# A state-space stage with its rotation sums on TensorE, merged products and phase rounding on ScalarE

## The chip, the cores and the metric

The kernel runs on one core of a Trainium2 chip. The metric is the device time of one execution in microseconds (us). Engines are written PE (TensorE matmul), PEld (TensorE weight load), DVE (VectorE), ACT (ScalarE), POOL (GpSimd) and SP (SyncE, which issues most DMAs). ACT and POOL issue some DMAs too; each engine works through its own instructions in order, so an instruction that waits holds up all that stand behind it on that engine.

## The reference, cut to what matters

The whole is a two-layer trunk of 256 time steps with 2048 channels: a state-space mixer with a gated linear unit (GLU) and a convolutional feed-forward network, then latent attention and a second feed-forward network. The change lies in the state-space mixer alone:

```
def s5_mixer(u, ...):                       # 128 groups of 16 channels, 64 complex states each
    mag = exp(dt * a_re)
    ab = mag * (cos(dt * a_im) + i sin(dt * a_im))
    bb = ((ab - 1) / a) * b
    h[t] = ab * h[t-1] + bb @ u[t]          # per group, complex, 256 steps
    y[t] = Re(c @ h[t]) + d_skip * u[t]
    y = gelu(y)
    val, gate = split(y @ w_glu + b_glu)
    return val * sigmoid(gate)
```

All of it is in 32-bit floating point. The numerators of `bb` and the output factors enter as products of powers of `ab` with `b` and `c`.

## The kernel before

The state-space stage (function `s5`) treats the 128 groups in 16 blocks of 8. Within a block, time is cut into 32 pieces of 8 steps; one piece times 16 channels makes the 128 rows of a tile. Inside a piece the recurrence is a matrix product with a 128 x 128 Toeplitz matrix; between pieces the state is carried by a scan over 32 positions. The complex state is rotated by the phase of each piece first, so that the scan runs with the real magnitude alone, and rotated back afterwards.

One pass of the loop at L610 to L645 works on several blocks at once. For pass n it does, in the order of the code:

- `part_v(n-1)` (L431): U times the transposed first-stage factors ET give each piece's contribution to the state; ScalarE copies it out of PSUM into `vs` (the copies follow L527).
- `part_c(n-2)` (L431 again, tiles `TP,U` and `f,H`): the output sums, U times the Toeplitz tile TP plus the state H times the output factors f. Per group pair there are three terms: U by TP, H by f1, H by f2.
- `part_r(n-1)`: four transposes (L530, L531) put the state and its swapped halves into PSUM; L533 and L534 multiply them by the cosine and the sine frame (`co`, `si`), L535 adds, L541 is the scan whose result is R.
- `part_k(n)`: U (L483), the block's kernel sums K from f and the loaded factors bc (L431, tiles `f,bc`), the skip diagonal (L438), a copy of K to DRAM (`kd`, on ScalarE's queue) and from there four loads in Toeplitz form (TP, L503, on SyncE's queue).
- `fetch(n+3)` (L460): the factor tile bc of a later block, 256 KB on ScalarE's queue, three buffers.
- `part_e(n)` (L514): eight transposes of the first-stage factors e.
- `part_h(n-1)`: a matmul with a swap matrix (L546) exchanges the halves of R in PSUM; L548 multiplies R by the cosine, L549 the swapped R by the sine, and L555 subtracts: H, written into columns 1 to 31 of each 32.
- `lead_f(n+1)`: the two output-factor products f1 and f2 (L454, 1024 elements a partition each), and in every second block the frames: L412 multiplies phase by position, L413 rounds by adding and taking off a large constant, L414 subtracts the rounded part, then Abs, Sin, Sin on ScalarE (L415 to L417).
- `lead_e(n+2)`: the two first-stage products e (L454 too), summed by an accumulating DMA from GpSimd (L468). Every fourth block `powers` (up to L405) makes the power factors `zs` for four blocks, which four ScalarE copies lay out.

Between these pieces `advance` puts steps of the GLU product of the blocks that are already done: 24 matmuls of 512 columns each (L254, L255, L257), with ScalarE and VectorE splitting the weights into two parts (L76, L77) and VectorE adding partial sums (L280). The first such step follows the fourth block; GLU weights come in 1 MB loads on SyncE's queue. `part_d` applies Gelu (L582) and transposes (L586) every four blocks.

The order of the instructions on each engine is not that of the code: a scheduler in the framework decides it when the program is built. A tile's buffer count, given with the tile, sets when it may be written again. The products are DVE's, the sums PE's; what links them here is H, which PE needs in `part_c` of the following pass, and f, which waits for the last reader of its buffer, `part_c` of three blocks earlier.

Of the kernel before, what the change touches and what calls it, by code (L numbers as in the profile page):

```python
# [47 lines left out]
def tile_trunk(ctx: ExitStack, tc: tile.TileContext, a: dict):  # L48
# [234 lines left out]
    def s5(f):  # L283
        with tc.tile_pool(name="s5", bufs=2) as q1, tc.tile_pool(name="dr", bufs=2, space=bass.MemoryType.DRAM) as dr:
# [61 lines left out]
            for K in Ks:  # L346
                pool.memset(K[:, 2 * P :], 0.0)
            Ds = [T(q1, [P, 8, 32], F32, f"dc{i}", 1) for i in range(2)]
# [32 lines left out]
            def powers(qt):  # L381
                ps_ = slice(32 * qt, 32 * qt + 32)
                z = T(q1, [P, 2, 9, 2, 32], F32, "z", 1)
                pool.memset(z[:, 0, 8, 1, :], 1.0)
                pool.memset(z[:, 1, 8, 1, :], 0.0)
                act.activation(z[:, :, 8, 0, :], cf[:, :, ps_], AF.Copy)
                act.activation(z[:, :, 0, 1, :], L[8][:, :, ps_], AF.Copy)
                for k, o, i, m in ((1, 7, 8, 1), (2, 5, 7, 2), (4, 1, 5, 4)):

                    def v(b):  # L390
                        return z[:, :, b : b + m].rearrange("p c m t n -> p c (m t) n")

# [8 lines left out]
                zz = T(q1, [P, 4, 8, 32], F32, "zs")  # L401
                act.activation(zz[:, 1], z[:, 1, 0:8, 1, :], AF.Copy, scale=cst[:, C_SG : C_SG + 1])
                act.activation(zz[:, 2], z[:, 0, 1:9, 0, :], AF.Copy, scale=cst[:, C_NSG : C_NSG + 1])
                act.activation(zz[:, 3], z[:, 1, 1:9, 0, :], AF.Copy, scale=-1.0)
                act.activation(zz[:, 0], z[:, 0, 0:8, 1, :], AF.Copy)  # L405
                return zz

            def frames(k):
                ps_ = slice(FR * NP * k, FR * NP * (k + 1))
                m, n = T(q1, [P, FR * NP, 32], F32, "si"), T(q1, [P, FR * NP, 32], F32, "co")  # L410
                cv = cst[:, C_CV : C_CV + 32].unsqueeze(1).to_broadcast([P, FR * NP, 32])
                dve.tensor_tensor(m, th[:, ps_].unsqueeze(2).to_broadcast([P, FR * NP, 32]), cv, op=ALU.mult)  # L412
                dve.tensor_scalar(n, m, MAGIC, MAGIC, op0=ALU.add, op1=ALU.subtract)  # L413
                dve.tensor_tensor(m, m, n, op=ALU.subtract)  # L414
# [3 lines left out]
                return [z.rearrange("p (k n) c -> k p (n c)", k=FR) for z in (m, n)]  # L418
# [31 lines left out]
            def product(tag, bufs, sb, i):  # L450
                h = (sb % PB) * NP
                o = T(q1, [P, NP, 8, 16], F32, tag, bufs)
                zt = zs[sb // PB][:, i, :, h : h + NP].rearrange("p i n -> p n i").unsqueeze(3).to_broadcast([P, NP, 8, 16])
# [8 lines left out]
            def lead_e(n):  # L462
# [4 lines left out]
                E[n], e2 = product("e1", 3, n, 0), product("e2", 2, n, 1)  # L467
                pool.dma_start(E[n], e2, accum_op=ALU.add)  # L468

            def lead_f(n):  # L470
                if n >= nb:
                    return
                F[n] = product("f1", 3, n, 2), product("f2", 3, n, 3)
                if n % FR == 0:
                    si, co = frames(n // FR)
                    for k in range(FR):
                        fr[n + k] = (si[k], co[k])
# [47 lines left out]
            def part_r(sb, vs, si, co):  # L525
# [6 lines left out]
                w1, w2 = T(q1, [P, W], F32, "w1"), T(q1, [P, W], F32, "w2")  # L532
                dve.tensor_tensor(w1, pvt, co, op=ALU.mult)  # L533
                dve.tensor_tensor(w2, pvs, si, op=ALU.mult)  # L534
                dve.tensor_tensor(w1, w1, w2, op=ALU.add)  # L535
# [8 lines left out]
            def part_h(sb, R, si, co):  # L544
# [3 lines left out]
                dve.tensor_tensor(h1, R, co, op=ALU.mult)  # L548
                dve.tensor_tensor(h2, prs, si, op=ALU.mult)  # L549
# [5 lines left out]
                dve.tensor_tensor(H[:, :, 1:32], cc(h1), cc(h2), op=ALU.subtract)  # L555
                return H

            def part_c(sb, yg, ff, U, TP, H):
                def h(g, j):
                    return H[:, 4 * g + j, :]  # L560
# [3 lines left out]
                    *((h, lambda g, j, z=z: flat2(z[:, 4 * g + j])) for z in ff),  # L564
# [31 lines left out]
            todo, zs, bc, E, F, fr, U, TP, ET, H = [], {}, {}, {}, {}, {}, {}, {}, {}, {}  # L596
# [13 lines left out]
            for n in range(nb + 2):  # L610
# [7 lines left out]
                if 0 <= n - 1 < nb:  # L618
                    R = part_r(n - 1, vs, *fr[n - 1])
# [14 lines left out]
                if 0 <= n - 1 < nb:  # L634
                    H[n - 1] = part_h(n - 1, R, *fr.pop(n - 1))
# [628 lines left out]
```

## Time and profile before

| what | value |
|---|---|
| median of 3 runs | 2123.69 us (2121.5 to 2124.83) |
| the profiled execution's own time | 2123.76 us |
| its span, first to last instruction | 2122.0 us |
| mean granted TensorE clock | 0.990 |
| busy over the span: PE, PEld | 2045.2 us, 1754.5 us |
| busy over the span: DVE, ACT, POOL | 1375.1 us, 1091.3 us, 31.0 us |
| DMA moved | 392.15 MB, mean 185 GB/s |
| share of the chain that ended last: PE, DVE, DMA, ACT | 88%, 5%, 3%, 2% |

The state-space stage is the first 236 us of the span or so. Its scans stand at 43.6, 53.3, 69.7, 78.9 and 86.0 us (blocks 0 to 4), then at 106.9, 117.8, 129.9, 146.1, 162.6, 172.8, 184.3, 194.7, 210.0, 218.5 and 229.3 us. A row of a timeline gives start, length, engine, line, operation, the tile written and the tiles read, shape and count; a length is that of a pipelined operation, so the step from one row's start to the next is what it costs on a busy engine. On PE one fp32 matmul of the 32-column-wide form is two records, so x16 stands for eight matmuls. An entry `[4.25 <-DVE H L555]` is idle time of the engine just before, and what ended it. A row of the windows view gives, for one stretch, each engine's busy time with its instructions in brackets, then the granted clock, the busy share of the DMA engines and the GB/s. A row of waits gives the sum of the waiting time, the number of waits and the longest.

### The profile page before, as it was taken

How to read it: one execution, taken by the hardware profiler on the slowest of the kernel's cores; microseconds unless marked ns; L12 is line 12 of the kernel's file. 1: busy time of each engine (PE TensorE's matmuls, PEld its weight loads, DVE VectorE, ACT ScalarE, POOL GpSimd, SP SyncE). 2: the span in 40 equal slices, each digit the busy share in tenths (PEclk: the TensorE clock that was granted, in tenths of full speed). 3: DMA queues.
4: the chain of work that ended last, by engine and by line, in shares of the span. 5: the costliest groups of instructions: out<-in, count | busy, mean ns of one | idle time of the engine just before them, and what ended most of it. 6: DMA issues, size and time to landing. Idle time of an engine off the chain costs nothing.

```text
span 2122.0 us, 30720 instructions
## 1 busy us (share of the span) xinstructions
PE 2045.2 (96%) x12372; PEld 1754.5 (83%) x12372; DVE 1375.1 (65%) x1935; ACT 1091.3 (51%) x1680; POOL 31.0 (1%) x73
## 2 busy tenths in 40 slices
PE   3789999999999999999999999999999999999998
PEld 2567788988888888888888998898888888888886
DVE  8889677665566556656785666656546655665566
ACT  6565456554455345534564555555445544554453
POOL 1000000000000000000000000000000000000000
PEclk9899999999999999999999999999999999999999
DMA  5777775755565565556444445475555655555642
GB/s 148 199 189 212 244 254 166 250 187 180 199 197 179 185 200 190 179 196 197 139 149 163 125 144 177 163 257 186 187 201 181 196 181 198 184 194 179 198 159 80
DMA packets 292255, 392.15 MB, mean 185 GB/s; under 512 B 10256, under 2 KB 205456, under 8 KB 291600
## 3 DMA queue, kind: packets, MB, share of 16 engines
q1 hardware_dynamic: 285632, 374.45, 53.7%
q0 software_dynamic: 2304, 8.39, 2.3%
q10 hardware_dynamic: 4176, 7.34, 1.0%
q8 instruction: 97, 1.59, 0.3%
q14 instruction: 46, 0.38, 0.1%
HBM read 375.73 MB, written 6.03 MB: 180 GB/s over the span
## 4 chain that ended last, share of the span: by engine, by line
PE 88%; DVE 5%; DMA 3%; ACT 2%; issue 1%; POOL 0%; SPq 0%; ACTq 0%; DVEq 0%; POOLq 0%
PE wk L758 29%; PE wk L760 15%; PE acc L115 9%; PE acc L114 9%; PE acc L113 9%; PE wk L113 2%; PE wk L114 2%; PE wk L115 2%; PE acc L255 2%; PE acc L254 2%; PE acc L257 2%; PE wk L431 2%; PE wk L255 1%; PE wk L257 1%; PE wk L254 1%
## 5 line engine op out<-in xcount | busy, mean ns | idle before, releaser
L77 DVE TENSOR_TENSOR wlo<-raw,whi 128x1024 fp32r<-128x1024 f32 (+1 forms) x590 | 699.6, 1188 | 543.7 <-ACT whi L76 540.3
L76 ACT ACTIVATE whi<-raw 128x1024 fp32r<-128x1024 f32 (+1 forms) x590 | 605.8, 1029 | 667.0 <-PE wk L758 298.5
L758 PE MATMUL wk<-act,whi 128*128 128x512 f32 x2688 | 674.0, 393 | 0.0
L758 PEld LDWEIGHTS wk<-act,whi 128*128 128x128 f32 x2688 | 484.6, 189 | 86.3
L760 PEld LDWEIGHTS wk<-act,wlo 128*128 128x128 f32 x2688 | 366.9, 191 | 26.1
L760 PE MATMUL wk<-act,wlo 128*128 128x256 f32 x2688 | 375.0, 283 | 0.0
L115 PE MATMUL acc<-whi,hl 128*128 128x512 f32 x636 | 249.8, 394 | 0.0
L114 PE MATMUL acc<-wlo,hh 128*128 128x512 f32 x636 | 249.4, 392 | 0.0
L113 PE MATMUL acc<-whi,hh 128*128 128x512 f32 x636 | 247.1, 389 | 0.0
L114 PEld LDWEIGHTS acc<-wlo,hh 128*128 128x128 f32 x636 | 119.5, 188 | 27.5
L113 PEld LDWEIGHTS acc<-whi,hh 128*128 128x128 f32 x636 | 119.5, 188 | 26.4 <-ACT hh L76 0.5
L115 PEld LDWEIGHTS acc<-whi,hl 128*128 128x128 f32 x636 | 119.9, 188 | 23.9
L830 DVE SCALAR_TENSOR_TENSOR cv<-gs,cw,cv 128x255 f32<-128x255 f32 (+1 forms) x168 | 81.0, 482 | 17.2 <-ACT cv L828 14.2
L828 ACT ACTIVATE cv<-gs,cb,cw 128x256 f32<-128x256 f32 x84 | 49.9, 594 | 45.6 <-DVE gs L766 45.6
L254 PE MATMUL acc<-whi,act 128*128 128x512 f32 x156 | 65.5, 420 | 3.8 <-ACT act L76 3.8
L77 DVE TENSOR_TENSOR wlo<-x,whi 128x1024 fp32r<-128x1024 f32 x40 | 48.8, 1223 | 26.7 <-ACT whi L76 26.0
L255 PE MATMUL acc<-whi,act 128*128 128x512 f32 x156 | 63.0, 404 | 1.1 <-DVE act L77 1.1
L76 ACT ACTIVATE whi<-x 128x1024 fp32r<-128x1024 f32 x40 | 42.3, 1061 | 37.6 <-PE wk L758 16.4
L114 PE MATMUL acc<-wlo,act 128*128 128x512 f32 (+1 forms) x152 | 55.0, 362 | 1.0 <-DVE wlo L106 0.9
L113 PE MATMUL acc<-whi,act 128*128 128x512 f32 (+1 forms) x152 | 54.1, 358 | 0.3 <-ACT whi L105 0.3
L115 PE MATMUL acc<-whi,act 128*128 128x512 f32 (+1 forms) x152 | 54.0, 356 | 0.0
L257 PE MATMUL acc<-wlo,act 128*128 128x512 f32 x156 | 49.2, 397 | 0.0
(314 smaller groups left out, 2558.1 us busy)
## 6 DMA issues: line engine op xcount, KB each, us to landing
raw<-in_w_up SPq DMA_DIRECT2D x86, 1024.0 KB
raw<-in_w_gate SPq DMA_DIRECT2D x84, 1024.0 KB
raw<-in_w_down SPq DMA_DIRECT2D x84, 1024.0 KB
raw<-in_w_glu SPq DMA_DIRECT2D x21, 1024.0 KB
x<-in_w_glu SPq DMA_DIRECT2D x11, 1024.0 KB
raw<-in_w_o SPq DMA_DIRECT2D x9, 1024.0 KB
e<-e POOLq DMA_DIRECT2D x16, 512.0 KB, 6.1
TP<-kd SPq DMA_DIRECT2D x64, 128.0 KB
```

What stands on the lines that cost most here:

```text
L76: act.activation(hi, src, AF.Copy)
L77: (eng or dve).tensor_tensor(lo, src, hi.bitcast(F32), op=ALU.subtract)
L113: pe.matmul(o, lh, rh, start=first, stop=False)
L114: pe.matmul(o, lh, rl, start=False, stop=False)
L115: pe.matmul(o, ll, rh, start=False, stop=last)
L254: pe.matmul(bank, ah, wh[:, k, :], start=first and k == 0, stop=False)
L255: pe.matmul(bank, al, wh[:, k, :], start=False, stop=False)
L257: pe.matmul(bank, acts(tb, 4 * b + j + k)[0], wl[:, k, :], start=False, stop=last and k == hk - 1)
L758: pe.matmul(o, w, pair(kt), start=kt == 0, stop=False)
L760: pe.matmul(o[:, 0, :], w, pair(kt)[:, 0], start=False, stop=kt == KT - 1)
L828: act.activation(cv[:, ft, :], gv[:, ft, :], AF.Identity, scale=cw[:, 2, n : n + 1], bias=cb[:, n : n + 1])
L830: dve.scalar_tensor_tensor(cv[:, ft, sh:], gv[:, ft, : S - sh], cw[:, 2 - sh, n : n + 1], cv[:, ft, sh:], op0=ALU.mult, op1=ALU.add,)
```

## The change

Four things are rewritten in `s5`.

1. The difference that made H is no longer taken on VectorE. H becomes two tiles, R times cosine and the swapped R times sine, and the output sums have four terms of f by H in place of two. The minus sign goes into the swap matrix, negated once by ScalarE (`swap`).
2. `part_r` multiplies both PSUM halves by both frames in one operation of 512; `si` and `co` stand in one tile `cs` for that.
3. f1 and f2 come from one operation of 2048 (tag `f1`); the power factors `zs` are laid out by block for that, and ScalarE's copies write them in that layout. The e products stay two operations (`single`).
4. The frames are cut in two. `angles` (phase by position on VectorE, then ScalarE adds the rounding constant, Identity with bias and scale -1) stands in `lead_f`; `frames` (one VectorE operation in place of L413 and L414, then Abs, Sin, Sin) stands in `lead_r` of the following pass.

```diff
-            Hs = [T(q1, [P, 8, 32], F32, f"H{i}", 1) for i in range(2)]
-            for z in Ds + Hs:
+            Hs = [[T(q1, [P, 8, 32], F32, f"H{i}{k}", 1) for k in range(2)] for i in range(2)]
+            swap = T(q1, [P, P], F32, "swap", 1)
+            act.activation(swap, cst[:, C_PS : C_PS + P], AF.Copy, scale=-1.0)
+            for z in Ds + [z for pair in Hs for z in pair]:
...
-            def frames(k):
...
-                dve.tensor_tensor(m, th[:, ps_].unsqueeze(2).to_broadcast([P, FR * NP, 32]), cv, op=ALU.mult)
-                dve.tensor_scalar(n, m, MAGIC, MAGIC, op0=ALU.add, op1=ALU.subtract)
-                dve.tensor_tensor(m, m, n, op=ALU.subtract)
+            def angles(k):
+                both = T(q1, [P, FR, 2, NP * 32], F32, "cs")
...
+                act.activation(n, m, AF.Identity, bias=magic, scale=-1.0)
+                return both, m, n
+
+            def frames(both, m, n):
+                dve.scalar_tensor_tensor(m, n, MAGIC, m, op0=ALU.subtract, op1=ALU.add)
                 act.activation(n, m, AF.Abs)
                 act.activation(m, m, AF.Sin, scale=cst[:, C_TPI : C_TPI + 1])
                 act.activation(n, n, AF.Sin, bias=half_pi, scale=-TWO_PI)
...
             def product(tag, bufs, sb, i):
+                o = T(q1, [P, 2 * NP, 8, 16], F32, tag, bufs)
...
-                E[n], e2 = product("e1", 3, n, 0), product("e2", 2, n, 1)
+                E[n], e2 = single("e1", 3, n, 0), single("e2", 2, n, 1)
...
-                F[n] = product("f1", 3, n, 2), product("f2", 3, n, 3)
+                F[n] = product("f1", 3, n, 2)
                 if n % FR == 0:
-                    si, co = frames(n // FR)
+                    an[n // FR] = angles(n // FR)
+
+            def lead_r(n):
+                if n < nb and n % FR == 0:
+                    both = frames(*an.pop(n // FR))
...
-                w1, w2 = T(q1, [P, W], F32, "w1"), T(q1, [P, W], F32, "w2")
-                dve.tensor_tensor(w1, pvt, co, op=ALU.mult)
-                dve.tensor_tensor(w2, pvs, si, op=ALU.mult)
-                dve.tensor_tensor(w1, w1, w2, op=ALU.add)
+                w = T(q1, [P, 2, W], F32, "w", 1)
+                dve.tensor_tensor(w, pvv.rearrange("p (i w) -> p i w", i=2), cs, op=ALU.mult)
+                w1 = w[:, 0]
+                dve.tensor_tensor(w1, w1, w[:, 1], op=ALU.add)
...
-                pe.matmul(prs, cst[:, C_PS : C_PS + P], R, start=True, stop=True)
-                h1, h2 = T(q1, [P, W], F32, "w1"), T(q1, [P, W], F32, "w2")
-                dve.tensor_tensor(h1, R, co, op=ALU.mult)
-                dve.tensor_tensor(h2, prs, si, op=ALU.mult)
+                pe.matmul(prs, swap, R, start=True, stop=True)
...
-                dve.tensor_tensor(H[:, :, 1:32], cc(h1), cc(h2), op=ALU.subtract)
+                dve.tensor_tensor(H[0][:, :, 1:32], cc(R), cc(cs[:, 0]), op=ALU.mult)
+                dve.tensor_tensor(H[1][:, :, 1:32], cc(prs), cc(cs[:, 1]), op=ALU.mult)
...
-                    *((h, lambda g, j, z=z: flat2(z[:, 4 * g + j])) for z in ff),
+                    *((h(i), lambda g, j, z=z: flat2(z[:, 4 * g + j])) for z in ff for i in range(2)),
...
                     ET[n] = part_e(E.pop(n))
+                    lead_r(n)
```

What the scheduler makes of it is seen in the built order of two engines. The names end in numbers that tell one tile of a kind from the next; they run differently in the two programs. First TensorE, where block 6's output sums stand behind the next block's `part_v` (`ET,U`), before the change:

```order
L431 MATMUL wk_1378<-ET_1303,U_1270 32x128 x8
L431 MATMUL wk_1390<-TP_1114,U_1088 32x128 x4
L431 MATMUL wk_1390<-f_225_1002,H_49_190 32x128 x4
L431 MATMUL wk_1390<-f_226_1004,H_49_190 32x128 x4
L431 MATMUL wk_1390<-TP_1114,U_1088 32x128 x4
L431 MATMUL wk_1390<-f_225_1002,H_49_190 32x128 x4
L431 MATMUL wk_1390<-f_226_1004,H_49_190 32x128 x4
```

And the same place after it:

```order
L446 MATMUL wk_1420<-ET_1355,U_1322 32x128 x8
L446 MATMUL wk_1432<-TP_1153,U_1127 32x128 x4
L446 MATMUL wk_1432<-f_205_1034,H_50_192 32x128 x4
L446 MATMUL wk_1432<-f_205_1034,H_51_193 32x128 x4
L446 MATMUL wk_1432<-f_205_1034,H_50_192 32x128 x4
L446 MATMUL wk_1432<-f_205_1034,H_51_193 32x128 x4
L446 MATMUL wk_1432<-TP_1153,U_1127 32x128 x4
L446 MATMUL wk_1432<-f_205_1034,H_50_192 32x128 x4
L446 MATMUL wk_1432<-f_205_1034,H_51_193 32x128 x4
L446 MATMUL wk_1432<-f_205_1034,H_50_192 32x128 x4
L446 MATMUL wk_1432<-f_205_1034,H_51_193 32x128 x4
```

Sixteen matmuls of f by H stood in a block and 32 do now; the place in the order is the same.

Then VectorE around the scan of block 10, whose result is R (the order calls the scan SCALAR_TENSOR_TENSOR). Before, `e_437` is the second product of block 13, from a tile bc that ScalarE fetched one pass earlier:

```order
L534 TENSOR_TENSOR w_411_1942<-wk_1936,si_1688 128x256
L454 TENSOR_TENSOR f_432_2029<-zs_1874,bc_1617 128x1024
L535 TENSOR_TENSOR w_410_1941<-w_410_1941,w_411_1942 128x256
L454 TENSOR_TENSOR f_433_2031<-zs_1874,bc_1617 128x1024
L541 SCALAR_TENSOR_TENSOR R_1947<-dc_47_188,w_410_1941 128x256
L413 TENSOR_SCALAR co_2034<-si_2033 128x512
L548 TENSOR_TENSOR w_430_2024<-R_1947,co_1689 128x256
L414 TENSOR_TENSOR si_2033<-si_2033,co_2034 128x512
L454 TENSOR_TENSOR e_437_2043<-zs_1874,bc_1801 128x1024
L549 TENSOR_TENSOR w_431_2025<-wk_2022,si_1688 128x256
L280 TENSOR_TENSOR f_84<-acc_2008,f_84 128x512
L555 TENSOR_TENSOR H_49_190<-w_430_2024,w_431_2025 128x8x31
```

After it, `H_50` is R times cosine, `H_51` the swapped R times sine, and `e_413` and `e_414` are the products of block 14, from the tile bc_2069:

```order
L470 TENSOR_TENSOR f_385_2112<-zs_1946,bc_1686 128x2048
L559 TENSOR_TENSOR w_2029<-wk_2024,cs_1752 128x512
L561 TENSOR_TENSOR w_2029<-w_2029 128x256
L567 SCALAR_TENSOR_TENSOR R_2033<-dc_48_190,w_2029 128x256
L578 TENSOR_TENSOR H_50_192<-R_2033,cs_1752 128x8x31
L476 TENSOR_TENSOR e_413_2284<-zs_1946,bc_2069 128x1024
L579 TENSOR_TENSOR H_51_193<-wk_2108,cs_1752 128x8x31
L280 TENSOR_TENSOR f_84<-acc_2094,f_84 128x512
L476 TENSOR_TENSOR e_414_2286<-zs_1946,bc_2069 128x1024
```

The tile bc_2069 is fetched by ScalarE (L482) in this very pass, after that pass's kernel sums; the first product of block 14 now stands between the two halves of H. The other blocks whose scans have the numbers 5 to 11 are like it, with both e products between the halves in most. Of ScalarE's order one row is gone from the end of the stage: the table load ahead of the last Gelu.

More of the change, by code (lines that the diff above doesn't have):

```diff
@@ L400, in powers @@
                     dve.tensor_tensor(v(o)[:, 1], u[:, 1], w[:, 0], op=ALU.add)
[L401 to L405, printed above, removed]
+                zz = T(q1, [P, PB, 4, NP, 8], F32, "zs")
@@ new lines, in blocks, with factor @@
+                def blocks(v):
+                    return v.rearrange("p i (b n) -> p i b n", b=PB)
+                def factor(t):
+                    return zz[:, :, t].rearrange("p b n i -> p i b n")
+                act.activation(factor(1), blocks(z[:, 1, 0:8, 1, :]), AF.Copy, scale=cst[:, C_SG : C_SG + 1])
+                act.activation(factor(2), blocks(z[:, 0, 1:9, 0, :]), AF.Copy, scale=cst[:, C_NSG : C_NSG + 1])
+                act.activation(factor(3), blocks(z[:, 1, 1:9, 0, :]), AF.Copy, scale=-1.0)
@@ L406, in powers @@
+                act.activation(factor(0), blocks(z[:, 0, 0:8, 1, :]), AF.Copy)
                 return zz
-            def frames(k):
+            def angles(k):
                 ps_ = slice(FR * NP * k, FR * NP * (k + 1))
[L410 to L414, printed above, removed]
+                both = T(q1, [P, FR, 2, NP * 32], F32, "cs")
+                n, m = (both[:, :, i].rearrange("p k (n c) -> p k n c", c=32) for i in range(2))
+                cv = cst[:, C_CV : C_CV + 32].unsqueeze(1).unsqueeze(1).to_broadcast([P, FR, NP, 32])
+                dve.tensor_tensor(m, th[:, ps_].rearrange("p (k n) -> p k n", k=FR).unsqueeze(3).to_broadcast([P, FR, NP, 32]), cv, op=ALU.mult)
+                act.activation(n, m, AF.Identity, bias=magic, scale=-1.0)
+                return both, m, n
@@ L417, in frames @@
                 act.activation(n, n, AF.Sin, bias=half_pi, scale=-TWO_PI)
-                return [z.rearrange("p (k n) c -> k p (n c)", k=FR) for z in (m, n)]
+                return both
             FR = 2
@@ L450, in product, with single @@
             def product(tag, bufs, sb, i):
-                h = (sb % PB) * NP
+                o = T(q1, [P, 2 * NP, 8, 16], F32, tag, bufs)
+                zt = zs[sb // PB][:, sb % PB, i : i + 2].rearrange("p t n i -> p (t n) i")
+                bt = bc[sb][:, i : i + 2].rearrange("p t n q -> p (t n) q")
+                shape = [P, 2 * NP, 8, 16]
+                dve.tensor_tensor(o, zt.unsqueeze(3).to_broadcast(shape), bt.unsqueeze(2).to_broadcast(shape), op=ALU.mult)
+                return o[:, :NP], o[:, NP:]
+            def single(tag, bufs, sb, i):
                 o = T(q1, [P, NP, 8, 16], F32, tag, bufs)
-                zt = zs[sb // PB][:, i, :, h : h + NP].rearrange("p i n -> p n i").unsqueeze(3).to_broadcast([P, NP, 8, 16])
+                zt = zs[sb // PB][:, sb % PB, i].unsqueeze(3).to_broadcast([P, NP, 8, 16])
                 dve.tensor_tensor(o, zt, bc[sb][:, i].unsqueeze(2).to_broadcast([P, NP, 8, 16]), op=ALU.mult)
@@ L472, in lead_f @@
                     return
-                F[n] = product("f1", 3, n, 2), product("f2", 3, n, 3)
+                F[n] = product("f1", 3, n, 2)
                 if n % FR == 0:
-                    si, co = frames(n // FR)
+                    an[n // FR] = angles(n // FR)
+            def lead_r(n):
+                if n < nb and n % FR == 0:
+                    both = frames(*an.pop(n // FR))
                     for k in range(FR):
-                        fr[n + k] = (si[k], co[k])
+                        fr[n + k] = both[:, k]
             def part_k(sb, ff, bc4):
@@ L523, in part_v, with part_r @@
                 return vs
-            def part_r(sb, vs, si, co):
+            def part_r(sb, vs, cs):
                 pvv = wk()
@@ L618, in s5 @@
                 if 0 <= n - 1 < nb:
-                    R = part_r(n - 1, vs, *fr[n - 1])
+                    R = part_r(n - 1, vs, fr[n - 1])
                 if n < nb:
```

12 lines of the change are left out of this document (7 added, 5 removed).

## The prediction

> **What bounds the kernel now.** The windows view comes first, cut at the starts of scans 0, 5 and 15 of the state-space stage's 16 blocks, and at one single block (166.72 to 177.46). The stage fills the first 236 us of the span; what follows keeps its order.
>
> ```profile
> span 2122.0 us, 30720 instructions
> ```
>
> ```profile
> core 0: us, PE busy (x) PEld busy (x) DVE busy (x) ACT busy (x) POOL busy (x), PEclk, DMA share, GB/s
> 0.00:43.60 43.60, 9.72 (x122) 6.88 (x122) 35.00 (x76) 29.14 (x76) 6.25 (x22) 1.00 0.54 146
> 43.60:106.90 63.30, 45.90 (x638) 34.85 (x639) 55.60 (x97) 34.32 (x76) 4.54 (x7) 0.81 0.74 195
> 106.90:229.30 122.40, 113.30 (x1409) 91.28 (x1408) 109.83 (x171) 73.88 (x139) 7.25 (x12) 0.97 0.71 195
> 229.30:244.00 14.70, 11.72 (x88) 8.70 (x87) 7.91 (x12) 6.98 (x10) 0.00 (x0) 0.88 0.68 198
> 166.72:177.46 10.74, 10.74 (x146) 9.02 (x145) 10.74 (x18) 6.48 (x13) 0.86 (x1) 1.00 0.72 206
> ```
>
> The reader is to see three regimes. Up to 43.6 VectorE leads (35.00 busy against TensorE's 9.72). From 43.6 to 106.9, blocks 0 to 4 without the GLU matmuls, TensorE idles 63.30 - 45.90 = 17.4 us. From 106.9 to 229.3, when GLU matmuls fill the gaps, it idles only 122.40 - 113.30 = 9.1 us in ten blocks, and in the single block both TensorE and VectorE are busy for all 10.74 us, while ScalarE has 10.74 - 6.48 = 4.26 us to spare. So there a microsecond taken from VectorE is only worth something if TensorE was waiting for it, and a microsecond added to TensorE is paid.
>
> Then the timeline of that block and the next:
>
> ```profile
> 169.01 0.27 PE L531 MATMUL wk<-cst,vs 128*128 128x128 f32 x1
> ...
> 170.57 0.34 ACTq L460 DMA_DIRECT2D bc<-in_sBC  x1
> ...
> 178.15 0.62 PE L431 MATMUL wk<-f,H 128*32 128x128 f32 x16
> 178.58 0.41 PE L431 MATMUL wk<-TP,U 128*32 128x128 f32 x8
> ...
> 179.75 0.27 PE L531 MATMUL wk<-cst,vs 128*128 128x128 f32 x1
> ...
> 179.94 1.23 DVE L454 TENSOR_TENSOR f<-zs,bc 128x1024 f32<-128x1024 f32 x1
> ```
>
> VectorE's own rows, one after another without a gap, give the price of every kind of operation as the step from one start to the next:
>
> ```profile
> 187.32 0.42 DVE L555 TENSOR_TENSOR H<-w,w 128x248 f32<-128x248 f32 x1
> 187.64 2.37 DVE L77 TENSOR_TENSOR wlo<-raw,whi 128x1024 fp32r<-128x1024 f32 x2
> 189.91 0.70 DVE L280 TENSOR_TENSOR f<-acc,f 128x512 f32<-128x512 f32 x1
> 190.52 0.69 DVE L412 TENSOR_TENSOR si<-th,cst 128x512 f32<-128x512 f32 x1
> 191.12 1.23 DVE L454 TENSOR_TENSOR f<-zs,bc 128x1024 f32<-128x1024 f32 x1
> 192.25 0.43 DVE L533 TENSOR_TENSOR w<-wk,co 128x256 f32<-128x256 f32 x1
> 192.59 0.43 DVE L534 TENSOR_TENSOR w<-wk,si 128x256 f32<-128x256 f32 x1
> 192.92 1.23 DVE L454 TENSOR_TENSOR f<-zs,bc 128x1024 f32<-128x1024 f32 x1
> 194.05 0.43 DVE L535 TENSOR_TENSOR w<-w,w 128x256 f32<-128x256 f32 x1
> 194.38 0.43 DVE L413 TENSOR_SCALAR co<-si 128x512 f32<-128x512 f32 x1
> 194.72 0.70 DVE L541 TENSOR_TENSOR_SCAN R<-dc,w 128x256 f32<-128x256 f32 x1
> 195.32 0.68 DVE L414 TENSOR_TENSOR si<-si,co 128x512 f32<-128x512 f32 x1
> 195.90 0.43 DVE L548 TENSOR_TENSOR w<-R,co 128x256 f32<-128x256 f32 x1
> ```
>
> That is 1.13 us for 1024 elements (191.12 to 192.25), 0.60 for 512 (190.52 to 191.12), 0.34 for 256, 0.32 for 248 (187.32 to 187.64). Doubling 512 adds 0.53, so an operation carries about 0.07 us that does not grow with its size; merging two saves that.
>
> **The change part by part.** *Rotation sums on TensorE.* The output sums multiply f by H; with H in two tiles there are four such terms where there were two. The x16 row of f,H takes 178.58 - 178.15 = 0.43 us (27 ns a record) per half-block; the second term doubles both halves, so +0.86 us of TensorE a block. From 106.9 to 229.3 there are ten blocks: **+8.6**, with nothing to hide it in the block that is busy throughout, and at most 9.1 us of idle time elsewhere. From 43.6 to 106.9 there are five blocks, +4.3 of busy time against 17.4 idle: I take **+1**, between 0 and +4.3, since that idle time is there because TensorE waits for others. The block's last sums come in the tail.
>
> *VectorE's relief.* The subtraction L555 goes (0.32) and the two products shrink from 256 to 248 elements (0.02); the merged first-rotation product saves 0.67 - 0.60 = 0.07; the merged f product 0.07; the frames lose L413 and L414 (0.34 + 0.58) for one operation of about 0.60, 0.32 every second block. In all 0.34 + 0.07 + 0.07 + 0.16 = 0.64 us a block. In the first five blocks (3.2 in all), where VectorE is busy 55.60 of 63.30, I count **-2** (0 to -3.2). In the ten later ones (6.4 in all) it can only come out of TensorE's 9.1 idle: **-1.5** (0 to -5).
>
> *Moved first-stage products.* In the built order VectorE now comes to the e products, which read the bc tile fetched in the same iteration, between the two H products (H0 from R, H1 from TensorE's swapped R) in seven blocks, those after scans 5 to 11. Before, one of these blocks showed what that costs:
>
> ```profile
> 136.69 1.23 DVE L454 TENSOR_TENSOR e<-zs,bc 128x1024 f32<-128x1024 f32 x1 [4.69 <-DMA bc<-in_sBC]
> ...
> 139.76 1.08 PE L431 MATMUL wk<-f,H 128*32 128x128 f32 x16 [4.25 <-DVE H L555]
> ```
>
> VectorE waited 4.69 us for the transfer, H stood behind it, and TensorE lost 4.25 us for H. The chain of waits holds two lengths of that transfer:
>
> ```profile
> 127.72 8.87 DMA bc<-in_sBC
> ...
> 159.34 3.25 DMA bc<-in_sBC
> ```
>
> Counted from the last L531 of a block (169.01), the fetch is issued at +1.56 (170.57), so its data land at +4.8 to +10.4. VectorE reaches the first e at +0.19 (179.94 less 179.75) + 2.19 for the merged f + 0.60 + 0.33 + 0.60 for the scan + 0.32 for H0 = +4.2, ahead of the data each time. Behind the data stand two e products (2.26) and H1 (0.32), so H1 is ready at +7.4 to +13.0. TensorE wants it four matmuls, or eight records (0.22), after its first f,H, at 9.14 + 0.22 = +9.4. The loss is 0 to 3.6 us a block. One of the seven is the stall shown, which is paid already. For the other six I take 0.5 each, **+3** (0 to +22): the 8.87 belongs to the worst wait, a latency midway (6.06) would cost 0.8, and one a quarter of the way up costs none.
>
> *Rounding on ScalarE.* Eight Identity operations at the price of the frames' other ScalarE steps:
>
> ```profile
> L416 ACT ACTIVATE si<-si,cst 128x512 f32<-128x512 f32 x8 | 5.8, 722 | 0.1
> ```
>
> 0.72 us each, covered by ScalarE's 4.26 idle in a full block. If that cover is gone they delay the copies of vs, ahead of which they stand in three blocks: **+0.5** (0 to 3 x 0.72 = 2.2). In the start-up the frames' Abs and Sin and a table load now stand ahead of the zs copies, on which the first e products and sums wait: **+1** (0 to 0.72 x 2 + 1.28 = 2.7); that also covers the zs copies' new scattered layout, which no row shows. The negated swap matrix and two more cleared tiles are made in the start-up, where ScalarE is idle for 14.5 us and GpSimd for most: nothing, and under 0.72 if not hidden.
>
> *Tail.* After the last scan TensorE waits for Gelu, and Gelu for its table:
>
> ```profile
> 234.49 1.28 ACT L582 ACT_TABLE_LOAD   x1
> ```
>
> In the new order ScalarE has one load fewer, this one: -1.28. The last block also loses L555 (-0.32) and its two shorter products' 0.02, and pays its +0.86: **-0.8**.
>
> Sum: 8.6 + 1 - 2 - 1.5 + 3 + 0.5 + 1 - 0.8 = +9.8 us. The profiled execution took 2123.76 us (span 2122.0 and 1.76 around it), 0.07 from the median of 2123.69, so the forecast is **2133.5 us**.
>
> **The rivals.** *TensorE's idle time takes the matmuls in.* The 9.1 us of idle time in the ten blocks equal the 8.6 added. If TensorE's idle stretches, 4.25 in one piece, come from things that run on beside it, the matmuls queue up later but end in the same place, and 8.6 and the 1 go: 2133.5 - 9.6 = 2123.9. For it: sums are near. Against: the block at 166.72 has no idle time, and the largest stall has H at its root, which the added matmuls need too.
>
> *The waits for bc decide.* If the latency is near 8.87 in most of the six blocks, each costs 8.87 + 1.56 + 2.58 - 9.4 = 3.6 us, of which I have counted 0.5: six times 3.1 is +18.6, 2152. It decides from a latency of 5.3 us up (9.4 - 1.56 - 2.58). For it: the stall shown. Against: 3.25 in the other quoted transfer, and a later TensorE wants H1 later.
>
> *The clock rises in the first blocks.* The granted clock is 0.81 from 43.6 to 106.9, where TensorE idles much, and 0.97 after, where it idles little. If more work lifts it, products that VectorE waits for there come sooner:
>
> ```profile
> DVE w L533 <- PE wk L531: 5.5, 4, 2.9
> ```
>
> These are 5.5 us in the whole stage, in four waits, the longest 2.9. If all of them went, the +1 would become -5.5, the sum +3.3 and the time 2127.0. The Trainium skill, "TensorE: Matmul & The Clock Gate", Part 1, says that the clock is lifted by a window of steady matmul activity and falls back in idle windows; the two clocks agree with that. Against the gain: the added matmuls come in one short run a block and leave the long idle stretches, which wait for transfers that stay, as they are.
>
> *VectorE is the true bound (faster).* Busy TensorE is not TensorE at its peak: the records' lengths overlap (a 0.62 row every 0.43), and VectorE is busy without a gap in the same block. If matmuls only fill the time until VectorE's next product comes, the added ones run in slack and 0.64 a block is gained in fifteen blocks: -9.6, with the tail -0.8, and +1 and +2 (start-up, part of the bc waits) = -7.4, so 2116.4. The point where it decides is a TensorE with over 0.86 us of hidden slack a block. The Trainium skill, "Perfetto Trace Analysis", "Identifying the Most-Contended Engine", says that the share of time matmuls are busy is a poor measure and that of weight loads a good one. Against the busy column the row has weight loads for 91.28 of 122.40, 75%, which speaks for some slack; but the GLU matmuls that fill the blocks are themselves work that has to be done before the stage ends, and that makes me hold to the first case.
>
> **How the numbers follow.** Forecast (5 to 15 slower) 0.56; idle time absorbs 0.15; the clock rises 0.04; bc waits decide 0.12; VectorE bound 0.13. About 0.2% (4.2 us) is what a measurement of this kernel can tell from no change, so faster means under 2119.4 and slower over 2127.9. Faster 0.13, same 0.15 + 0.04 = 0.19, slower 0.56 + 0.12 = 0.68. The range reaches from the low side of the VectorE case to short of the full bc case, 2116 to 2148: half of the first (0.07) and most of the second (0.10) lie outside.
>
> **What would show it.** In the new trace: 32 records of f,H per half-block at 27 ns; blocks between scans 5 and 15 longer by about 0.9, TensorE still busy throughout; waits of e for bc after scans 5 to 11, and of f,H for H1, together near 3 us beyond the 4.25 shown; no table load ahead of the last Gelu. The forecast is wrong if scan 15 starts no later than before (229.3), if f,H records cost far from 27 ns, or if single blocks come out shorter than 10.74 us.

## The result, and the profile after

The changed kernel takes 2151.43 us (median of four runs, 2148.41 to 2153.86) against 2123.93 us: a ratio of 1.0129, 95% interval 1.0118 to 1.0141. That is 27.5 us slower. The forecast was 2133.5, with a range from 2116 to 2148: the prediction was wrong. The profiled execution is the shortest of the four, 2148.41 us, 24.6 more than the one of before. First its span, then its stretches, cut again at the starts of scans 0, 5 and 15, with the last block before scan 15 by itself:

```profile
span 2146.6 us, 31704 instructions
```

```profile
core 0: us, PE busy (x) PEld busy (x) DVE busy (x) ACT busy (x) POOL busy (x), PEclk, DMA share, GB/s
0.00:44.70 44.70, 11.72 (x122) 8.96 (x122) 34.88 (x70) 29.66 (x76) 6.83 (x25) 1.00 0.52 140
44.70:114.30 69.60, 49.27 (x798) 39.34 (x799) 57.00 (x89) 41.10 (x87) 5.60 (x10) 0.83 0.69 181
114.30:253.90 139.60, 124.05 (x1728) 100.69 (x1727) 102.40 (x128) 74.67 (x136) 6.21 (x9) 0.96 0.61 172
253.90:268.60 14.70, 12.69 (x122) 9.95 (x121) 7.57 (x11) 5.75 (x9) 0.00 (x0) 0.90 0.63 190
242.30:253.90 11.60, 11.60 (x145) 9.80 (x141) 6.17 (x9) 4.56 (x8) 0.00 (x0) 1.00 0.53 154
```

Held against the rows of before: the start takes 44.7 us instead of 43.6 (+1.1), blocks 0 to 4 take 69.6 instead of 63.3 (+6.3), the ten blocks after them 139.6 instead of 122.4 (+17.2), and from scan 15 to the end it is 1892.7 both times. These make the 24.6. In the ten blocks TensorE has 319 more records (1728 less 1409; 320 were added) and is busy 10.75 us longer (more than the 8.6 that the records cost at 27 ns each), but it also idles 15.55 us instead of 9.1, while VectorE, with 7.4 us less work (102.40 against 109.83), is idle for 37.2 us instead of 12.6.

What VectorE waited for longest, from 30 us to the end of the stage (sum, number of waits, longest), before and after:

```profile
DVE e L454 <- DMA bc<-in_sBC: 5.5, 2, 4.7
```

```profile
DVE e L476 <- DMA bc<-in_sBC: 21.4, 8, 4.9
```

And what TensorE waited for, before:

```profile
PE wk L546 <- DVE R L541: 10.3, 5, 5.4
...
PE wk L431 <- DVE H L555: 4.3, 1, 4.3
...
PE wk L431 <- DVE f L454: 2.8, 1, 2.8
```

And after:

```profile
PE wk L572 <- DVE R L567: 16.6, 4, 8.4
PE wk L446 <- DVE f L470: 7.7, 1, 7.7
PE wk L540 <- ACT yg L591: 6.0, 5, 2.3
...
PE wk L446 <- DVE H L579: 2.8, 2, 1.6
```

The e products wait for bc eight times where it was twice. I had TensorE wait for H1 in consequence, and it did so for only 2.8 us. It lost its time elsewhere, and in each stretch to something else. The wait for f is over before scan 0. The four waits for the scan's result R all lie in blocks 0 to 4, and the longest of them comes from a late bc by a way that I had not seen: an e product stands ahead of the scan there.

```profile
85.03 1.23 DVE L476 TENSOR_TENSOR e<-zs,bc 128x1024 f32<-128x1024 f32 x1 [4.93 <-DMA bc<-in_sBC]
86.18 0.68 DVE L567 TENSOR_TENSOR_SCAN R<-dc,w 128x256 f32<-128x256 f32 x1
...
87.01 1.19 PE L572 MATMUL wk<-R,swap 128*128 128x256 f32 x2 [8.44 <-DVE R L567]
```

In the ten blocks after scan 5 TensorE's largest wait is the one for ScalarE's copy of the output sums (yg, L591): 5.3 us of the 6.0, in four waits. The list of before has none for this copy. The chain of waits shows how a late bc leads there, here in the pass after scan 9 (start, length, what):

```profile
173.84 4.73 DMA bc<-in_sBC
178.66 2.36 DVE e L476 x2
181.02 0.32 DVE H L579
...
181.86 0.68 DVE cs L424
182.54 1.14 DVE wlo L77
183.68 0.60 DVE f L280
184.28 0.61 DVE cs L429
184.91 0.63 ACT cs L430
185.56 1.28 ACT L431
186.94 0.34 ACTq L482
```

The transfer ends; both e products, H1, the angles (L424), a weight split, a partial sum and the rounding (L429) run one after the other on VectorE; only then can ScalarE do Abs (L430) and load the table for Sin (L431), and the next thing on the chain is ScalarE's issue of the next bc fetch (L482). So a late bc holds up the issue of the next one, three times, from 112.23, 137.19 and 173.84 on. A circle that keeps itself going is not shown: for the three transfers so held up (issued at 124.78, 152.40 and 186.94) the e products waited 0.85, 3.06 and 1.22 us, and the chain goes on by ScalarE's copies to TensorE. The timeline two blocks later, where no fetch follows any more, shows what it costs TensorE:

```profile
206.00 2.36 DVE L476 TENSOR_TENSOR e<-zs,bc 128x1024 f32<-128x1024 f32 x2 [3.66 <-DMA bc<-in_sBC]
...
208.74 0.86 PE L446 MATMUL wk<-f,H 128*32 128x128 f32 x24 [1.12 <-DVE H L579]
...
212.25 0.63 ACT L430 ACTIVATE cs<-cs 128x512 f32<-128x512 f32 x1 [1.17 <-DVE cs L429]
...
214.16 0.36 ACT L591 ACTIVATE yg<-wk 128x256 f32<-128x256 f32 x1
...
214.57 1.09 PE L540 MATMUL wk<-cst,e 128*128 128x128 f32 x8 [1.60 <-ACT yg L591]
```

TensorE pays 1.12 us for H1, and 1.60 more for a copy of the output sums (yg, L591) that stands behind Abs and the two Sin on ScalarE.

### The profile page after: what moved, and what is told of

It is laid out like the page before. It is cut to its first block, busy times and chain, and to the rows that moved or that the text cites. A ratio compares the mean times of both kernels' runs of the same rounds, so it can differ in the third digit from the quotient of the medians.

```text
span 2146.6 us, 31704 instructions
## 1 busy us (share of the span) xinstructions
PE 2062.3 (96%) x12884; PEld 1769.6 (82%) x12884; DVE 1369.0 (64%) x1879; ACT 1098.7 (51%) x1687; POOL 31.6 (1%) x76
## 4 chain that ended last, share of the span: by engine, by line
PE 86%; DVE 6%; ACT 3%; DMA 3%; issue 1%; POOL 0%; SPq 0%; ACTq 0%; DVEq 0%; POOLq 0%
PE wk L783 29%; PE wk L785 15%; PE acc L115 9%; PE acc L114 9%; PE acc L113 9%; PE wk L446 2%; PE wk L113 2%; PE wk L115 2%; PE wk L114 2%; PE acc L254 1%; PE acc L255 1%; DMA bc<-in_sBC 1%; PE acc L257 1%; DVE wlo L77 1%; DVE e L476 1%
## 5 line engine op out<-in xcount | busy, mean ns | idle before, releaser
L855 DVE SCALAR_TENSOR_TENSOR cv<-gs,cw,cv 128x255 f32<-128x255 f32 (+1 forms) x168 | 81.0, 482 | 17.2 <-ACT cv L853 14.3
L476 DVE TENSOR_TENSOR e<-zs,bc 128x1024 f32<-128x1024 f32 x32 | 38.4, 1220 | 22.3 <-DMA bc<-in_sBC 21.4
```

The lines of the kernel that those rows point to most:

```text
L476: dve.tensor_tensor(o, zt, bc[sb][:, i].unsqueeze(2).to_broadcast([P, NP, 8, 16]), op=ALU.mult)
L855: dve.scalar_tensor_tensor(cv[:, ft, sh:], gv[:, ft, : S - sh], cw[:, 2 - sh, n : n + 1], cv[:, ft, sh:], op0=ALU.mult, op1=ALU.add,)
```

## The experiments

Theories set up against each other first: **A**, the waits for bc make most of the loss; **B**, the added matmuls cost much more than I counted; **C**, the frames on ScalarE do it. Later ones: **D**, the frames again; **E**, the merged f product; **F**, only part 1 matters. Each ratio is against the kernel before in the same session, with its 95% interval; 0.1% is 2.1 us. "Early fetch" stands for one edit: the half of bc that the e products and K read becomes a tile of its own, fetched a pass earlier. The other half, which f reads, becomes a second tile, fetched a pass later than before, so each transfer is 128 KB instead of 256; no trace shows VectorE waiting for the second tile. The arithmetic stays the same. What the edit is worth is therefore the worth of all this, and of the order that the scheduler then makes.

**1. The changed kernel with the early fetch.**

```diff
-                    bc[n] = T(q1, [P, 4, NP, 16], F32, "bc", 3)
-                    eng.dma_start(bc[n], a["sBC"][n])
+                    bc[n] = T(q1, [P, 2, NP, 16], F32, "bc", 4)
+                    eng.dma_start(bc[n], a["sBC"][n][:, 0:2])
+
+            def fetch_f(n, eng):
+                if n < nb:
+                    bf[n] = T(q1, [P, 2, NP, 16], F32, "bf", 2)
+                    eng.dma_start(bf[n], a["sBC"][n][:, 2:4])
...
-                    fetch(n + 3, act)
+                    fetch(n + 4, act)
+                    fetch_f(n + 2, act)
```

> The changed kernel, but the halves of bc are two tiles, and the half that the e products read is fetched one pass earlier (four buffers); all is computed as in the reference. Theory A (the waits of VectorE for bc, in a loop from fetch over e, H1, frames and the ScalarE queue to the next fetch, make most of the loss): the e products come after H1 or find their data there, VectorE's waits for bc fall from 21.4 us to under 4, and the time to 2130 to 2136. Theory B (the doubled output sums cost TensorE far more than the 8.6 us that I counted, the waits are hidden beside them): 2145 to 2152, waits gone all the same. Theory C (the frames, now rounded on ScalarE, stand ahead of ScalarE's copies and hold TensorE up): 2142 to 2152, with TensorE's waits for ScalarE (yg, U, vs) still near the 12.8 us of the changed kernel between scans 5 and 15.

2138.52 us, ratio 1.0073 (1.0059 to 1.0086). The time lies between A and B/C: the fetch is worth 12.9 us of the 27.5 by the medians, and 14.4 stay. VectorE's waits of e for bc fell to 5.1 us, not under 4. Against C, TensorE's waits for ScalarE between scans 5 and 15 fell too, from 12.8 to 5.6 us. The two stretches after scan 0, to be held against 69.60 and 139.60 us:

```profile
45.00:112.30 67.30, 49.83 (x803) 38.82 (x804) 57.36 (x84) 41.58 (x87) 5.60 (x10) 0.85 0.70 189
112.30:242.90 130.60, 120.69 (x1723) 97.75 (x1722) 102.17 (x133) 74.17 (x136) 6.22 (x9) 0.99 0.66 182
```

Of the 9.0 us that the ten blocks got back, 5.6 are idle time of TensorE (15.55 to 9.91). The other 3.4 are busy time (124.05 to 120.69) for nearly the same records, beside a granted clock of 0.99 in place of 0.96.

**2. The kernel before with the same edit.**

> The kernel before, with the same early fetch of the e half of bc. Theory A: the stall of 4.69 us at block 8 goes, so 2117 to 2122, some 2 to 6 faster than before. Theories B and C: the stall was hidden, 2122 to 2125.

2124.54 us, ratio 0.9999 (0.9990 to 1.0008). Nothing: the stall of 4.69 us that I had put on the path in the prediction costs the kernel before nothing that can be measured (the interval excludes a gain of over 2.1 us). TensorE's wait of 4.3 us for H is gone from the trace, but its waits for the copy vs grew from 2.6 to 9.1 us. So the late fetch is dear only in company.

**3. The kernel before with doubled sums by zeros**: TensorE's extra work alone.

```diff
+            Hz = T(q1, [P, 8, 32], F32, "Hz", 1)
+            pool.memset(Hz, 0.0)
...
-                    *((h, lambda g, j, z=z: flat2(z[:, 4 * g + j])) for z in ff),
+                    *((k, lambda g, j, z=z: flat2(z[:, 4 * g + j])) for z in ff for k in (h, lambda g, j: Hz[:, 4 * g + j, :])),
```

> The kernel before, with TensorE's part of the change alone: each f by H matmul is followed by one of f by a tile of zeros, so the sums are unchanged and VectorE keeps its work. In the built order of this kernel too the e products stand ahead of H in the blocks after scans 5 to 11. Theory A: VectorE waits over 12 us for bc and the time is 2140 to 2150. Theory B: 2143 to 2150, too, but with waits that TensorE does not feel. Theory C: 2131 to 2135, the price of the matmuls alone.

2143.66 us, ratio 1.0089 (1.0076 to 1.0102). Its waits, VectorE's first:

```profile
DVE e L456 <- DMA bc<-in_sBC: 10.9, 5, 3.5
```

```profile
PE wk L433 <- DVE H L557: 9.4, 6, 3.0
```

No operation of VectorE was changed here, yet the scheduler put the e products of blocks 9 to 15 ahead of H, and here TensorE does wait for H, 9.4 us in six waits. It is the mechanism of my rival "the waits for bc decide", called up by the matmuls alone.

**4. The same with the early fetch.**

> The same doubled sums by zeros, with the early fetch of the e half of bc. Theory A: the price of the matmuls alone shows, 0.86 us in each of ten to sixteen blocks, so 8.6 to 13.8 over the kernel before with the early fetch: 2127 to 2134. Theory B: the matmuls cost over 18 us, 2139 to 2148. Theory C: 2127 to 2134, as by A, so only the changed kernel with the early fetch tells A from C.

2131.75 us, ratio 1.0042 (1.0030 to 1.0055): the matmuls alone cost 7.2 us over experiment 2 by the medians, 8.9 over the kernel before by this ratio. B falls, and A stands as the larger part: with the fetch late the same matmuls cost 19.6. What the changed kernel pays beyond is another 6.8 us (2138.52 less 2131.75), and no theory so far had it right.

**5. The changed kernel, early fetch, frames in one piece** (`frames` as before, in `lead_f`, no `lead_r`).

> The changed kernel with the early fetch (2138.5), and the frames again in one piece with the rounding on VectorE, as before. Left to explain are about 7 us: 14.4 over the kernel before, less the 7.2 that the doubled sums cost by themselves with the early fetch. They lie in the first five blocks (67.3 us against 61.1). Theory D (the frames' steps on ScalarE, cut in two, stand ahead of the zs copies and of U and K there): 2131 to 2134. Theory E (the merged f product waits for its whole buffer, 7.4 us of VectorE waiting for the output sums): no change, 2136 to 2141. Theory F (the sums and the shorter H chain meet badly, only part 1 matters): 2136 to 2141.

2137.71 us, ratio 1.0053 (1.0041 to 1.0066), against 1.0073 (1.0059 to 1.0086): the intervals overlap, and the time is not in D's range. D falls as the cause of the whole rest; a smaller share (0.8 us by the medians, 4 by the ratios) is not excluded.

**6. The changed kernel, early fetch, f as two products in two tiles.**

```diff
-                F[n] = product("f1", 3, n, 2)
+                F[n] = single("f1", 3, n, 2), single("f2", 3, n, 3)
```

> The changed kernel with the early fetch (2138.5), and f again as two products of 1024 in two tiles (the layout of zs stays). Theory E: VectorE's waits of f for the output sums fall from 7.4 us to under 2, the time to 2131 to 2134. Theories D and F: 2138 to 2140, the 0.07 us a block that merging saves lost again.

2131.37 us, ratio 1.0032 (1.0021 to 1.0042): 7.1 us back. E: the merge that I had booked as a gain of 0.07 us a block is a loss.

**7. The changed kernel, early fetch, one H tile with the subtraction on VectorE** (part 1 undone).

> The changed kernel with the early fetch (2138.5), and H again one tile with the subtraction on VectorE. By the price of the matmuls (7.2, less what the longer VectorE chain costs back) 2131 to 2134 by theories D and E; by F everything goes, 2123 to 2126.

2126.61 us, ratio 1.0007 (0.9996 to 1.0019): 11.9 us less than experiment 1, more than the matmuls' 7.2. The time lies just above F's range, so this run alone could not refute F. It falls by experiment 6, which got 7.1 us back with part 1 in place.

**8. Only the merged products (parts 2 and 3), early fetch.**

> Only the merged products of the change (one first-rotation product, one f product, zs laid out by block) with the early fetch: sums and frames as before. Theory D: the merged products are a small gain, 2121 to 2124 against 2124.5 of the kernel before with the early fetch. Theory E: 2129 to 2132. Theory F: 2121 to 2124.

2128.93 us, ratio 1.0027 (1.0016 to 1.0037). The merged products cost 4 to 6 us with no added matmul anywhere, near what E wanted. This run does not tell the merged f from the merged rotation product; 7 against 10 does.

**9. The changed kernel, its own fetch, f as two products.**

> The changed kernel, fetch as it is there, with f again as two products in two tiles. If the merged f product costs its 7.1 us (2138.5 to 2131.4 with the early fetch) by itself, on top of the waits for bc: 2142 to 2146. If it only costs where the early fetch has rearranged the order: 2149 to 2153. VectorE's waits for bc stay over 12 us in both.

2146.65 us, ratio 1.0109 (1.0094 to 1.0123), between the two expectations and 4.8 us under the changed kernel by the medians, short of the 7.1; the intervals, 1.0094 to 1.0123 and 1.0118 to 1.0141, overlap a little. VectorE's waits for bc stayed at 15.7 us.

**10. The merged rotation product and the rounding on ScalarE (parts 2 and 4), early fetch;** parts 1 and 3 undone as in 7 and 6.

> What is left of the change once the two parts that cost are undone: the merged first-rotation product and the rounding on ScalarE, with the early fetch; sums with the subtraction on VectorE, f as two products. If costs add: 2126.6 less some 3 (the waits for f's buffer in that kernel) to 7 (the difference that the two products made beside the doubled sums), so 2119 to 2124, at best 5 under the kernel before. If frames on ScalarE cost what the merged rotation product gains: 2124 to 2127.

2119.36 us, ratio 0.9981 (0.9971 to 0.9990): faster than both kernels, 4.6 us under the one before. It differs from experiment 7 only in f as two products, and that is worth 7.3 us. In its trace the larger gain is in blocks 0 to 4 (58.5 us, 63.3 before); in its ten blocks TensorE idles 6.5 us, against 9.1, and from scan 15 to the end it takes 2.8 us longer:

```profile
43.30:101.80 58.50, 45.96 (x637) 32.80 (x638) 53.61 (x89) 38.46 (x81) 4.54 (x7) 0.85 0.78 206
101.80:222.10 120.30, 113.82 (x1409) 91.10 (x1408) 109.35 (x159) 77.59 (x143) 7.24 (x12) 0.99 0.73 202
```

**11. The kernel before, early fetch, tripled sums** (the zero tile twice).

> The kernel before with the early fetch, and two sums by zeros beside each f by H: twice the added matmuls of the kernel with doubled sums (2131.75, 7.2 over 2124.5). If TensorE is the bound from scan 5 on, and the first five blocks' idle time takes in the rest: another 7 to 9, 2139 to 2141. If part of the first doubling was hidden in idle time that is now used up: 10 to 14 more, 2142 to 2146. If the cost was waits and order and not matmuls: 2130 to 2136.

2141.60 us, ratio 1.0089 (1.0075 to 1.0103), 9.9 us over the doubled sums, between the first two expectations. The last block before scan 15 shows the price bare, in the kernel before and in this one:

```profile
218.50:229.30 10.80, 10.80 (x113) 9.02 (x110) 6.74 (x12) 4.55 (x8) 0.00 (x0) 1.00 0.57 168
```

```profile
232.50:245.00 12.50, 12.50 (x179) 10.71 (x174) 6.70 (x12) 4.55 (x8) 0.00 (x0) 1.00 0.49 149
```

10.8 us with single sums, 11.6 with double ones (the changed kernel's last row above), 12.5 with triple ones, at 113, 145 and 179 records: 0.8 and 0.9 for some 32 more records each. That is the 0.86 of the prediction.

**12. Part 1 alone on the kernel before, early fetch.**

> Part 1 alone on the kernel before, with the early fetch: four terms of f by H, no subtraction. Against the doubled sums by zeros (2131.75) VectorE has 0.34 us a block less to do. If that is worth what I counted in the prediction (half or less of it, in all blocks 0 to 3 us): 2129 to 2132. If VectorE is the bound: 5.4 less, 2126. If the shorter chain to H1 is worth nothing: 2131 to 2134.

2127.62 us, ratio 1.0019 (1.0010 to 1.0028), against 1.0042 (1.0030 to 1.0055) with the subtraction kept: dropping it and the two longer products is worth 4.1 us by the medians, most of the 5.4 that VectorE's rows add up to. I had counted half or less. Whether VectorE's time or the shorter way from R to H makes it is not told apart.

**13. The changed kernel, early fetch, f in one tile but written by two operations.**

```diff
-                dve.tensor_tensor(o, zt.unsqueeze(3).to_broadcast(shape), bt.unsqueeze(2).to_broadcast(shape), op=ALU.mult)
+                for t in range(2):
+                    c = slice(NP * t, NP * (t + 1))
+                    s1 = [P, NP, 8, 16]
+                    dve.tensor_tensor(o[:, c], zt[:, c].unsqueeze(3).to_broadcast(s1), bt[:, c].unsqueeze(2).to_broadcast(s1), op=ALU.mult)
```

> The changed kernel with the early fetch (2138.5), f still one tile of 2048 with one buffer of three, but written by two operations of 1024. If the buffer held as one piece makes the 7.1 us that two tiles win (2131.4): no change, 2136 to 2141. If the length of the one operation (2.2 us, ahead of the rotation product on VectorE) makes it: 2130 to 2134.

2131.80 us, ratio 1.0041 (1.0029 to 1.0054): the buffer held as one piece, E's first reason, is not it; the single operation is. Block 3 of experiment 1, where the last transpose (L562) starts at 77.36:

```profile
77.08 2.29 DVE L470 TENSOR_TENSOR f<-zs,bf 128x2048 f32<-128x2048 f32 x1 [0.97 <-PE wk L446]
...
77.36 0.27 PE L562 MATMUL wk<-cst,vs 128*128 128x128 f32 x1
...
79.29 0.68 DVE L564 TENSOR_TENSOR w<-wk,cs 128x512 f32<-128x512 f32 x1
...
79.98 1.23 DVE L476 TENSOR_TENSOR e<-zs,bc 128x1024 f32<-128x1024 f32 x1
...
81.46 1.22 DVE L476 TENSOR_TENSOR e<-zs,bc 128x1024 f32<-128x1024 f32 x1
82.59 0.68 DVE L572 TENSOR_TENSOR_SCAN R<-dc,w 128x256 f32<-128x256 f32 x1
...
83.42 1.19 PE L577 MATMUL wk<-R,swap 128*128 128x256 f32 x2 [3.48 <-DVE R L572]
```

And the same block here, where it starts at 77.63:

```profile
77.63 0.27 PE L565 MATMUL wk<-cst,vs 128*128 128x128 f32 x1
...
77.94 0.69 DVE L567 TENSOR_TENSOR w<-wk,cs 128x512 f32<-128x512 f32 x1 [0.18 <-PE wk L565]
...
78.55 1.22 DVE L473 TENSOR_TENSOR f<-zs,bf 128x1024 f32<-128x1024 f32 x1
...
80.01 1.22 DVE L473 TENSOR_TENSOR f<-zs,bf 128x1024 f32<-128x1024 f32 x1
81.15 0.68 DVE L575 TENSOR_TENSOR_SCAN R<-dc,w 128x256 f32<-128x256 f32 x1
...
81.89 0.70 PE L580 MATMUL wk<-R,swap 128*128 128x256 f32 x2 [1.67 <-DVE R L575]
```

With one operation the rotation product starts 1.93 us after the transpose, because f has just begun; with two it starts 0.31 after. Behind it two products of 1024 stand ahead of the scan in both blocks, the e products in one and the halves of f in the other, so the scan comes 5.23 us after the transpose in one and 3.52 in the other. TensorE's wait for R is 3.48 in one and 1.67 in the other. Over the 16 blocks the mean from the last transpose to the rotation product is 1.86 us with the one operation, 1.01 with the two, and 0.85 in the kernel before. The edit also let the scheduler place the e products elsewhere, so the gain is that of a changed order as well. Nor is this delay all that a merged f can cost: in experiment 8 the same mean is 0.81 us, and the kernel is 4.4 us slower than experiment 2 all the same. What it loses there stays open.

**14. Parts 1 and 2, early fetch.**

> The four-term sums and the merged first-rotation product with the early fetch; frames as before, f as two products. Between part 1 alone (2127.6) and parts 1, 2 and 4 (2131.4). If the rotation product is what meets the sums badly: 2131 to 2134. If the frames on ScalarE are: 2126 to 2128, the 0.07 us a block of the merge gained.

2128.84 us, ratio 1.0029 (1.0020 to 1.0038), between its two ranges.

**15. Parts 1 and 4, early fetch.**

> The four-term sums and the frames with the rounding on ScalarE, with the early fetch; the first-rotation products as two operations, f as two products. If the frames meet the sums badly: 2131 to 2134. If the rotation product does: 2125 to 2128, 0.16 us a block gained on part 1 alone (2127.6).

2132.22 us, ratio 1.0042 (1.0028 to 1.0056), by the median in the range for the frames. But with part 1 alone at 1.0019 (1.0010 to 1.0028), 14 at 1.0029 and parts 1, 2 and 4 at 1.0032 (1.0021 to 1.0042), neither is set apart from its neighbours. Which of parts 2 and 4 meets the four-term sums badly stays open.

**16. Experiment 10 with bc fetched as before.**

> The faster version (2119.4: merged rotation product and rounding on ScalarE, sums and f as before) with bc fetched as in the kernel before. If the e products again stand close behind their fetch and VectorE waits for bc: 2123 to 2128. If they come late enough: 2118 to 2121.

2122.52 us, ratio 0.9999 (0.9989 to 1.0008): the gain of 10 shows only with the early fetch (the two intervals just touch), though the kernel before gets nothing from it. VectorE waits once for bc here, 3.4 us.

## Why the prediction was wrong, step by step

Two steps of the sum failed. The first is "I take 0.5 each, +3": the waits for bc, with the order that goes with them, were worth 12.9 us, and they reached TensorE mostly by other ways than H1. The second is "merging two saves that": the merged f, booked as a small gain, cost about 7 us. Undoing both gives back 20.1 us (2151.43 to 2131.37, experiment 6). What is left is 7.4 us by the medians and 6.8 by the ratio, and the forecast without its +3 is +6.8. That this rest agrees is partly luck: its terms do not agree one by one.

- **The price of the matmuls (right for the matmuls alone).** 0.86 us a block; 0.8 and 0.9 were measured in a bare block, and 7.2 to 8.9 us in all (experiment 4) against 8.6 + 1.
- **VectorE's relief (too small for the subtraction, wrong sign for f).** Of the 0.64 us a block, the 0.34 of part 1 was nearly all worth it (4.1 of 5.4). For f, "merging two saves that" failed: the sum went by the length of the operation and not by what stands behind it. The 2.2 us of f stood ahead of the rotation product, on the chain from transposes over scan and swap matmul, and one operation in place of two cost about 7 us (experiments 6 and 13). I had it in the sum of the e products' start time (2.19 ahead of L559) and did not ask what it did to the scan.
- **The waits for bc (right mechanism as a rival, mis-sized in the forecast).** I counted +3 and gave +18.6 more as a rival with a chance of 0.12. With and without the early fetch the waits are worth 12.9 us. I underrated two things: the earlier blocks also wait (one of the eight waits, and TensorE idles 8.44 us for the R behind it), and a late bc passes on through the frames to ScalarE's copies. The rival's time, 2152, is near the 2151.4 measured by luck: it had nothing of f's 7 us, and its term for the waits, 21.6 in all, was 8.7 too large. It also reasoned by TensorE waiting for H1, which came to 2.8 us in the changed kernel (9.4 in experiment 3).
- **The frames on ScalarE (small).** +0.5 was counted for the Identity; what I missed is that Abs, Sin and Sin now wait for VectorE with the copy of the output sums behind them (1.60 us shown above). Where bc comes early this goes: TensorE's waits for that copy in the ten blocks are 5.3 us in the changed kernel and 0.3 in experiment 1. By itself the part is not a loss: experiment 5 is not told apart from 1.
- **The start (right size, wrong cause).** +1 was forecast for frames ahead of the zs copies, +1.1 measured. But with f in two and the frames left as they are, scan 0 goes from 44.7 us in the changed kernel to 43.1 (experiment 9), and from 44.9 (experiment 7) to 43.3 (experiment 10), where the kernel before has 43.6. By these traces it is the merged f product again.
- **The tail (-0.8 forecast, 0.0 measured).** The table load ahead of the last Gelu went, as expected, and TensorE's wait of 0.85 us for that Gelu with it, but the time from scan 15 to the end is the same.
- **TensorE's idle time as a cover (refuted).** In the changed kernel the idle time of the ten blocks grew, from 9.1 to 15.55 us, with the waits for bc in it. Nearly without them (experiment 4 has one, of 2.0 us) the doubled sums made TensorE busy 10.6 us longer in the ten blocks than in experiment 2, and its idle time there only fell from 12.05 to 10.97.
- **The clock (refuted here).** The granted clock in blocks 0 to 4 went from 0.81 to 0.83, and the stretch became longer; in the ten blocks it fell from 0.97 to 0.96. The Trainium skill, "TensorE: Matmul & The Clock Gate", Part 1, which has the clock fall back in idle windows, is not contradicted: the idle stretches were still there, 20.3 us in blocks 0 to 4.
- **VectorE as the bound (refuted as a whole, half right in the small).** VectorE's idle time in the ten blocks trebled while the blocks grew longer; but what part 1 took off VectorE was nearly all worth it (experiment 12). On the busy column my doubt was misplaced: in a block with TensorE busy throughout, each added record showed up at its price. The Trainium skill, "Perfetto Trace Analysis", "Identifying the Most-Contended Engine", calls that column a poor measure of how close a kernel is to the roofline. Whether work can be added for nothing is another question, and for that one it told rightly, in the bare block (10.8 of 10.8 busy, weight loads 9.02, 84%), that there was no slack.

What stays open: costs do not add. Part 1 costs 3.1 us by itself (experiment 12 over 2) but 12.0 on top of parts 2 and 4 (6 over 10); the merged f costs 7.1 and 7.3 in two settings (1 over 6, 7 over 10). Each edit makes the scheduler place other instructions anew; that part 1's price depends on that placing is likely, and not shown.

## What to carry to other kernels

Price an operation on an in-order engine not by its length alone but by what stands behind it when it starts: two halves that let a short link of the chain slip in between can beat one merged operation, and here they did by about 7 us. When work is added to a full engine, look in the built order for what the scheduler now moves ahead of the critical instruction on the other engines; a load that was early enough becomes late, and fetching it a pass earlier cost nothing here (experiment 2). Undo a change part by part before dropping it: two of its four parts, with that earlier fetch, made the kernel 0.19% faster than before.

## What was not expected of the hardware

A bc fetch of 256 KB, among the 1 MB weight loads, stood for 4.73 us on the chain of the changed kernel (6.79 from 137.19 on), 0.4 to 0.6 of an 11.6 us block: a fetch and its first use in the same pass left VectorE waiting seven times between scans 5 and 15, 16.5 us in all. The kernel before had one such wait of 4.69 us, and taking it away gained nothing (0.9990 to 1.0008).
